# A product of 512 columns for the high and low parts of an activation, and side steps held in program order

## The chip, the cores and the metric

One core of a Trainium2 chip runs the whole program in one launch. The metric is the device time of an execution in microseconds (us). The kernel before takes 3224.32 us, the median of 3 runs (3224.06 to 3224.76). Engines are named as in the profile: PE is TensorE's products, PEld its loads of the stationary operand, DVE is VectorE, ACT is ScalarE, POOL is GpSimd and SP the engine that issues the loads.

## The reference

Two transformer blocks on 256 tokens of width 2048, all in float32. The first block is an SSD (Mamba-2) and an attention branch, then a product-key expert layer (`peer`): each token takes 8 heads x 16 of 16384 experts, found by a top-16 of the sums of two top-16 lists.

```python
def peer(h, wq, k1, k2, u, v):
    q = (t @ wq).reshape(T, PEER_HEADS, 2, PEER_KEY_DIM // 2)
    ...
    v1, i1 = lax.top_k(s1, PEER_TOPK)
    v2, i2 = lax.top_k(s2, PEER_TOPK)
    ...
    sc, pos = lax.top_k(cand, PEER_TOPK)
    g = jax.nn.softmax(sc, axis=-1)
    ...
        act = jax.nn.gelu(jnp.einsum('thkd,td->thk', u[ib], tb), approximate=False)
        return jnp.einsum('thk,thkd->td', gb * act, v[ib])
```

The second block is an attention with a relative bias from a table (`rel_bias`), a convolution branch, a cross attention on a memory of 256 rows (`mem`) and an MLP of 8192 hidden units, `square(relu(nm @ w1)) @ w2`.

## The kernel before

**Products.** A float32 product is made of three on rounded parts: each weight tile is split into a high part (`whi`, a cast by ACT, line 114) and a low part (`wlo`, the remainder, by DVE, line 115), the activation likewise (`hTh`, `hTl`), and high x high, high x low and low x high are summed in PSUM. One split covers 128 x 1024 weights; a raw tile of 1 MB is loaded by SP's queue into one of 3 buffers (`raw`) and gives two splits; `whi` and `wlo` have 3 buffers each.

**Two block forms.** `gemm_block` (line 147) holds 128 columns of the activation stationary and streams 512 weight columns. `gemm_cols` (lines 174 to 176) holds 128 weight columns stationary and streams the activation's 256 tokens: three products of 256 columns for each K tile and each 128 weight columns, in blocks of 512 weight columns, 192 products a block. It serves `up` of the expert layer (8 stages e of 4 blocks, all 16384 experts densely) and `w1` of the MLP (16 blocks). The token weights go in afterwards: `gate` multiplies the activations (written to DRAM as `act`, read back as `ag`) with a dense table of gate weights (`gd`, read in pieces of 64 bytes), and `down` is 8 stages of 4 `gemm_block`s.

**Order.** Blocks are written one after the other; work of other kinds is cut into steps (generators) and a rate says how many are put between the groups of a block (`step(rate)`): `routing` (top-16 steps, softmax, then the one-hot products of `all_gates`) beside `wq` and `up`, `gate(e+1)` beside `down(e)`, and `ahead` (squares of `mem`, the bias table) beside `down(2)`. `evac` moves a finished block out of PSUM. This written order is only the start: a scheduler orders each engine's instructions by its own estimate of when they can run, so a side step may land earlier than it is written.

**Names for the steps below.** `top16`, `route` (lines 788 to 838), `gate` (944 to 961), `fetch` (932, up to three pieces ahead), `ahead` (977 to 1000), the MLP's `f` (1359).

## Time and profile before

| | |
|---|---|
| median of 3 runs | 3224.32 us |
| the profiled execution | 3223.47 us, its span 3221.7 us |
| mean granted clock of TensorE | 0.997 |
| PE, PEld busy | 99%, 86% of the span |
| DVE, ACT busy | 62%, 47% |
| up and its gates | about 522 to 1283 us |
| down | about 1285 to 2020 us |
| MLP | about 2492 us to the end |

A busy PE is not a PE at its peak, since products overlap and their ends are modelled; the number of products that start in a stretch says more. The clock is given as a share of 2.4 GHz, with 1.2 GHz as its other level.

### The profile page before, as it was taken

To read this page: it belongs to the slowest core of one execution; us is meant where nothing else is said; L and a number is where in the kernel's file an instruction comes from. 1 tells how busy PE (TensorE), PEld (TensorE's weight loads), DVE (VectorE), ACT (ScalarE), POOL (GpSimd) and SP (SyncE) were. 2 spreads that over 40 slices of the span, in tenths; PEclk is the share of its full clock that TensorE was granted. 3 is DMA by queue.
4 is the path that set the end of the run, shared out by engine and by line. 5 is a ranking of instruction groups with operands and counts; after the bars stand their busy time and mean duration, and the time that the engine had idled before them with its cause. 6 is when DMAs were issued, how large, how long until landed. Compare 5 with 4: busy or idle time off the path is not lost.

```text
span 3221.7 us, 45786 instructions
## 1 busy us (share of the span) xinstructions
PE 3183.3 (99%) x18818; PEld 2766.7 (86%) x18818; DVE 2004.5 (62%) x2812; ACT 1529.6 (47%) x1967; POOL 92.2 (3%) x126
## 2 busy tenths in 40 slices
PE   8999999999999999999999999999999999999998
PEld 7877788999999999777787778888888989899897
DVE  6665679955666654555555555799666555555555
ACT  6456555544444444444443444545656434444344
POOL 0000000000000010000100000000000000000000
PEclk9999999999999999999999999999999999999999
DMA  6544454565667786667666765555554555555554
GB/s 234 183 144 171 144 180 157 200 209 203 229 240 248 242 289 214 233 235 239 231 223 228 240 215 183 196 183 177 176 170 170 185 189 189 183 186 189 187 183 157
DMA packets 101475, 647.31 MB, mean 201 GB/s; under 512 B 11269, under 2 KB 12421, under 8 KB 32400
## 3 DMA queue, kind: packets, MB, share of 16 engines
q1 hardware_dynamic: 82512, 575.63, 51.7%
q0 software_dynamic: 18752, 68.74, 6.4%
q8 instruction: 147, 2.41, 0.3%
q14 instruction: 64, 0.52, 0.0%
HBM read 607.11 MB, written 37.22 MB: 200 GB/s over the span
## 4 chain that ended last, share of the span: by engine, by line
PE 72%; issue 15%; DVE 6%; DMA 4%; POOL 1%; ACT 1%; SPq 0%; ACTq 0%; POOLq 0%; DVEq 0%
PE acc L147 52%; PE acc L176 5%; PE acc L174 5%; PE acc L175 5%; DMA ag<-gd 3%; DVE wlo L115 2%; PE tp L214 1%; DVE scr L793 0%; POOL gd L898 0%; DVE i L828 0%; PE mm L743 0%; DVE hTl L959 0%; DMA raw<-in_peer_v_dram 0%; DMA raw<-in_mem_dram 0%; POOL act L915 0%
## 5 line engine op out<-in xcount | busy, mean ns | idle before, releaser
L115 DVE TENSOR_TENSOR wlo<-raw,whi 128x1024 fp32r<-128x1024 f32 x1064 | 1300.1, 1223 | 1041.8 <-ACT whi L114 1038.1
L114 ACT CAST whi<-raw 128x1024 fp32r<-128x1024 f32 x1064 | 1114.6, 1049 | 1455.2 <-PE acc L147 853.0
L147 PE MATMUL acc<-whi,hTh 128*128 128x512 f32 x2650 | 1061.7, 401 | 10.5 <-ACT whi L114 10.5
L147 PE MATMUL acc<-wlo,hTh 128*128 128x512 f32 x2650 | 1051.5, 397 | 7.0 <-DVE wlo L115 6.8
L147 PE MATMUL acc<-whi,hTl 128*128 128x512 f32 x2650 | 1050.8, 397 | 0.0
L176 PE MATMUL acc<-hTh,wlo 128*128 128x256 f32 x3072 | 866.8, 282 | 10.1 <-DVE wlo L115 9.9
L174 PE MATMUL acc<-hTh,whi 128*128 128x256 f32 x3072 | 868.0, 283 | 0.0
L175 PE MATMUL acc<-hTl,whi 128*128 128x256 f32 x3072 | 863.6, 281 | 0.0
L147 PEld LDWEIGHTS acc<-whi,hTh 128*128 128x128 f32 x2650 | 498.7, 188 | 132.7 <-ACT whi L114 10.9
L147 PEld LDWEIGHTS acc<-wlo,hTh 128*128 128x128 f32 x2650 | 499.0, 188 | 129.0 <-DVE wlo L115 13.2
L147 PEld LDWEIGHTS acc<-whi,hTl 128*128 128x128 f32 x2650 | 498.4, 188 | 120.7 <-issue 0.3
L176 PEld LDWEIGHTS acc<-hTh,wlo 128*128 128x128 f32 x3072 | 579.4, 189 | 14.9 <-DVE wlo L115 14.4
L174 PEld LDWEIGHTS acc<-hTh,whi 128*128 128x128 f32 x3072 | 579.8, 189 | 0.2
L175 PEld LDWEIGHTS acc<-hTl,whi 128*128 128x128 f32 x3072 | 579.7, 189 | 0.2
L1087 DVE SCALAR_TENSOR_TENSOR cc<-hc,vec,cc 128x256 f32<-128x256 f32 x240 | 102.1, 478 | 0.5
L955 DVE TENSOR_TENSOR ag<-ag 128x1024 f32<-128x1024 f32 x32 | 39.2, 1225 | 61.5 <-DMA ag<-gd 61.2
L958 ACT CAST hTh<-ag 128x1024 fp32r<-128x1024 f32 x32 | 32.9, 1050 | 31.7 <-DVE ag L955 22.5
L675 DVE TENSOR_TENSOR x<-acc,x 128x512 f32<-128x512 f32 x72 | 46.4, 681 | 0.3 <-PE acc L147 0.2
L911 DVE TENSOR_TENSOR at<-acc,rtok 128x512 f32<-128x512 f32 x64 | 43.7, 690 | 0.5
L959 DVE TENSOR_TENSOR hTl<-ag,hTh 128x1024 fp32r<-128x1024 f32 x32 | 38.5, 1222 | 1.6 <-ACT hTh L958 0.8
L915 POOL DMA_DIRECT2D act<-at x32 | 17.4, 545 | 741.4 <-ACT at L913 741.1
L940 POOL DMA_DIRECT2D ag<-gd x32 | 37.4, 1170 | 6.3 <-DMA gd<-gs 5.1
(314 smaller groups left out, 1496.3 us busy)
## 6 DMA issues: line engine op xcount, KB each, us to landing
raw<-in_peer_u_dram SPq DMA_DIRECT2D x128, 1024.0 KB, 4.9
raw<-in_peer_v_dram SPq DMA_DIRECT2D x128, 1024.0 KB, 4.9
raw<-in_w_dram SPq DMA_DIRECT2D x128, 1024.0 KB, 4.9
raw<-in_w_in_dram SPq DMA_DIRECT2D x83, 1024.0 KB, 4.9
raw<-in_w_out_dram SPq DMA_DIRECT2D x32, 1024.0 KB, 4.9
raw<-in_wq_dram SPq DMA_DIRECT2D x16, 1024.0 KB, 4.9
act<-at POOLq DMA_DIRECT2D x32, 512.0 KB, 4.3
gd<-gs POOLq DMA_DIRECT2D x16, 1024.0 KB, 5.6
```

What stands on the lines that cost most here:

```text
L114: nc.scalar.copy(hi[:, :kt, :n], raw[:, k0 : k0 + kt, :n])
L115: nc.vector.tensor_sub(lo[:, :kt, :n], raw[:, k0 : k0 + kt, :n], hi[:, :kt, :n].bitcast(F32))
L147: mm(o, a, b, start=start, stop=stop)
L174: mm(o, hi[:, k, cs], xh[:, kk], start=kk == 0 and c % 2 == 0, stop=False)
L175: mm(o, hi[:, k, cs], xl[:, kk], start=False, stop=False)
L176: mm(o, lo[:, k, cs], xh[:, kk], start=False, stop=kk == 15 and c % 2 == 1)
L675: nc.vector.tensor_add(x[:, t, sl], acc[t], x[:, t, sl])
L911: nc.vector.tensor_mul(at[:, 2 * c : 2 * c + 2], acc[c], rt)
L940: nc.gpsimd.dma_start(g, gd[e, :, :, nb * 4 : nb * 4 + 4])
L955: nc.vector.tensor_mul(av, av, g.rearrange("p b c t -> p c b t"))
L959: nc.vector.tensor_sub(wl[:, cs], a, wh[:, cs].bitcast(F32))
L1087: nc.vector.scalar_tensor_tensor(o, hc[:, c, tap : tap + T], w[:, tap : tap + 1], o, OP.mult, OP.add)
```

## The change

The activation's high and low parts lie side by side (`hT`, [K tile, 2, 256]), so that one product of 512 columns under a stationary `whi` gives high x high in the left half of a PSUM bank and high x low in the right; `wlo` gives one product of 256 columns into the left half. A block now has 256 weight columns, and the weights of `peer_u` and `w1` are laid out for it on the host. `sums` adds the two halves at the block's end: ACT copies the right half out, DVE adds the left. Side steps are held in the order in which they are written (`pin`). The bias table is made by one product and spread over partitions by DMA, and two empty steps stand between mem's load and its squares.

```diff
+        pin = tc.keep_in_program_order
...
-        def gemm_cols(xh, xl, src, evac, rate=2):
+        def gemm_cols(x2, src, evac, rate=2):
...
-            for g in range(4):
+            for g in range(2):
                 raw = load_w(src(g))
                 for k0 in range(0, 4, 2):
-                    hi, lo = split_w(raw, k0)
-                    for k in range(2):
-                        kk = 4 * g + k0 + k
-                        for c in range(4):
+                    hi, lo = (
+                        a.rearrange("p a (k n) -> p (a k) n", n=T) for a in split_w(raw, k0)
+                    )
+                    for k in range(4):
+                        kk = 8 * g + 2 * k0 + k
+                        for c in range(2):
                             cs = slice(c * P, c * P + P)
-                            o = acc[c // 2][:, c % 2 * T : c % 2 * T + T]
-                            mm(o, hi[:, k, cs], xh[:, kk], start=kk == 0 and c % 2 == 0, stop=False)
-                            mm(o, hi[:, k, cs], xl[:, kk], start=False, stop=False)
-                            mm(o, lo[:, k, cs], xh[:, kk], start=False, stop=kk == 15 and c % 2 == 1)
+                            mm(
+                                acc[c], hi[:, k, cs], x2[:, kk].rearrange("p a t -> p (a t)"),
+                                start=kk == 0, stop=False,
+                            )
+                            mm(acc[c][:, :T], lo[:, k, cs], x2[:, kk, 0], start=False, stop=kk == 15)
...
+        def sums(o, acc):
+
+            for c in range(2):
+                nc.scalar.copy(o[:, c], acc[c][:, T:])
+                nc.vector.tensor_add(o[:, c], acc[c][:, :T], o[:, c])
...
         def new_hT():
-            h = main.tile([P, KD, T], F32R, name="hTh", tag="hTh", bufs=2)
-            l = main.tile([P, KD, T], F32R, name="hTl", tag="hTl", bufs=2)
-            return h, l
...
+            x2 = main.tile([P, KD, 2, T], F32R, name="hT", tag="hT", bufs=2)
+            return x2[:, :, 0], x2[:, :, 1], x2
...
-            nc.vector.max(vals[:, 0:8], src)
+            z.pin(nc.vector.max(vals[:, 0:8], src))
...
-            nc.vector.tensor_scalar_mul(mx, sc[:, 0:1], -1.0)
+            z.pin(nc.vector.tensor_scalar_mul(mx, sc[:, 0:1], -1.0))
...
-                    nc.vector.tensor_tensor(four(B2), io, row(i2T, t), OP.is_equal)
+                    z.pin(nc.vector.tensor_tensor(four(B2), io, row(i2T, t), OP.is_equal))
...
             for nb in range(4):
-                def f(acc, nb=nb):
-                    at = pp.tile([P, 4, T], F32, name="at", bufs=2)
-                    for c in range(2):
-                        nc.vector.tensor_mul(at[:, 2 * c : 2 * c + 2], acc[c], rt)
-                    yield
...
+                at = pp.tile([P, 4, T], F32, name="at", bufs=2)
+                for b in range(2):
+
+                    def f(acc, nb=nb, b=b, at=at):
+                        z.sums(at[:, 2 * b : 2 * b + 2], acc)
+                        yield
+                        nc.vector.tensor_mul(at[:, 2 * b : 2 * b + 2], at[:, 2 * b : 2 * b + 2], rt)
+                        if b:
+                            nc.scalar.activation(at, at, AF.Gelu)
...
-                nc.vector.tensor_mul(av, av, g.rearrange("p b c t -> p c b t"))
+                z.pin(nc.vector.tensor_mul(av, av, g.rearrange("p b c t -> p c b t")))
                 yield
                 cs = slice(nb * 4, nb * 4 + 4)
-                nc.scalar.copy(wh[:, cs], a)
+                z.pin(nc.scalar.copy(wh[:, cs], a))
...
                 mn = z.load_w(A["mem"][:, t].rearrange("p (a b) -> p a b", b=512))
+                yield
+                yield
                 for b in range(4):
-                    z.sq_sum(mn[:, b], ssm[:, t, b : b + 1])
+                    z.pin(z.sq_sum(mn[:, b], ssm[:, t, b : b + 1]))
                     yield
...
+            bv = pp.tile([8, 384], F32)
+            yield
+            pb = z.mm_tile()
+            z.pin(mm(pb[:8, :384], rb, bk, start=True, stop=True))
...
-            for h in range(8):
-                pb = z.mm_tile()
-                mm(pb[:, :384], rb[:, h : h + 1].to_broadcast([33, P]), bk, start=True, stop=True)
-                bv = pp.tile([P, 384], F32, name="bv", bufs=2)
-                nc.scalar.copy(bv, pb[:, :384])
-                nc.gpsimd.dma_start(env["bd"][h], bv)
+            for h in range(0, 8, 4):
+                br = pp.tile([P, 4, 384], F32, name="br", tag="at", bufs=2)
+                nc.gpsimd.dma_start(br, bd1[h : h + 4].partition_broadcast(P))
+                nc.gpsimd.dma_start(env["bd"][h : h + 4].rearrange("h p j -> p h j"), br)
                 yield
```

The MLP's `f` changes as `up`'s does (`sums`, then relu and scale, square, split), in halves.

What this makes of the engines' order, at the places that matter. PE in an up block before (`acc0`, `acc1` are PSUM banks, `hTh`, `hTl` the activation's parts):

```order
L174 MATMUL acc1_11578<-hTh_2976,whi_11701 128x256
L175 MATMUL acc1_11578<-hTl_2977,whi_11701 128x256
L176 MATMUL acc1_11578<-hTh_2976,wlo_11702 128x256
L174 MATMUL acc0_11577<-hTh_2976,whi_11729 128x256
L175 MATMUL acc0_11577<-hTl_2977,whi_11729 128x256
L176 MATMUL acc0_11577<-hTh_2976,wlo_11730 128x256
```

PE in an up block of the change:

```order
L182 MATMUL acc1_7772<-hT_2974,wlo_7776 128x256
L178 MATMUL acc0_7771<-hT_2974,whi_7796 128x512
L182 MATMUL acc0_7771<-hT_2974,wlo_7797 128x256
L178 MATMUL acc1_7772<-hT_2974,whi_7796 128x512
L182 MATMUL acc1_7772<-hT_2974,wlo_7797 128x256
```

Two products stand where three stood, of 512 and of 256 columns.

DVE beside the routing before (L791 to L795 and L835 to L837 are top-16 and softmax steps):

```order
L837 RECIPROCAL sm_p_4014<-sm_p_4014 128x1
L793 MATCH_REPLACE scr_3354<-v_p_4019,scr_3353 128x128
L824 TENSOR_TENSOR eq_p_3963<-abf_p_3961,iok_3351 128x512
L794 MAX v_p_4019<-scr_3354 128x8
L827 TENSOR_TENSOR eq_p_3963<-eq_p_3963,if_p_3897 128x512
L795 MAX_INDEX iu_p_4020<-v_p_4019,scr_3354 128x8
L828 TENSOR_REDUCE i12_3350<-eq_p_3963 128x2x16
L115 TENSOR_TENSOR wlo_3827<-raw_3824,whi_3826 128x1024
```

DVE beside the routing in the change (L804 to L808, L850 and L852 are those steps, L194 the adds of `sums`):

```order
L118 TENSOR_TENSOR wlo_4963<-raw_4960,whi_4962 128x1024
L852 RECIPROCAL sm_p_4942<-sm_p_4942 128x1
L804 MAX v_p_4947<-scr_3350 128x8
L805 MAX_INDEX iu_p_4948<-v_p_4947,scr_3350 128x8
L806 MATCH_REPLACE scr_3350<-v_p_4947,scr_3350 128x128
L807 MAX v_p_4947<-scr_3350 128x8
L118 TENSOR_TENSOR wlo_4984<-raw_4960,whi_4983 128x1024
L808 MAX_INDEX iu_p_4948<-v_p_4947,scr_3350 128x8
L194 TENSOR_TENSOR at_4836<-acc0_4837,at_4836 128x256
L194 TENSOR_TENSOR at_4836<-acc1_4838,at_4836 128x256
```

Two heads' steps are mixed before, and one head's follow one another now. Counted by `wlo`, the softmax steps (`mx_p`) stand from the 135th to the 183rd before and from the 140th to the 240th now; the number of table switches on ACT in this part goes from 8 to 22.

ACT at the end of an up block in the change (`L193` copies the right half of a bank, `L117` is the cast to `whi`):

```order
L117 CAST whi_7895<-raw_7893 128x1024
L911 COPY gs_7758<-mm_7816 128x128x4
L911 COPY gs_7758<-mm_7826 128x128x4
L117 CAST whi_7919<-raw_7893 128x1024
L193 COPY at_7646<-acc0_7771 128x256
L117 CAST whi_7961<-raw_7959 128x1024
L193 COPY at_7646<-acc1_7772 128x256
L117 CAST whi_7981<-raw_7959 128x1024
```

The block of `acc0_7771` ends with `whi_7858`; two casts of the next block stand ahead of the first copy, one between the copies. Before, ACT had none of these copies there.

DVE in the first down stage before (`ag` is multiplied with its gates on L955):

```order
L955 TENSOR_TENSOR ag_13440<-ag_13440 128x1024
L115 TENSOR_TENSOR wlo_13407<-raw_13404,whi_13406 128x1024
L959 TENSOR_TENSOR hTl_13368<-ag_13440,hTh_13367 128x1024
L115 TENSOR_TENSOR wlo_13423<-raw_13404,whi_13422 128x1024
L955 TENSOR_TENSOR ag_13552<-ag_13552 128x1024
L115 TENSOR_TENSOR wlo_13450<-raw_13447,whi_13449 128x1024
L115 TENSOR_TENSOR wlo_13466<-raw_13447,whi_13465 128x1024
L924 SCALAR_TENSOR_TENSOR x_1801<-acc0_13297,x_1801 128x512
L924 SCALAR_TENSOR_TENSOR x_1801<-acc1_13298,x_1801 128x512
L955 TENSOR_TENSOR ag_13698<-ag_13698 128x1024
```

DVE in the first down stage of the change (L973 is that multiplication, L977 the low part after it):

```order
L973 TENSOR_TENSOR ag_11706<-ag_11706 128x1024
L118 TENSOR_TENSOR wlo_12009<-raw_12006,whi_12008 128x1024
L118 TENSOR_TENSOR wlo_12025<-raw_12006,whi_12024 128x1024
L942 SCALAR_TENSOR_TENSOR x_1799<-acc0_11857,x_1799 128x512
L942 SCALAR_TENSOR_TENSOR x_1799<-acc1_11858,x_1799 128x512
L118 TENSOR_TENSOR wlo_12043<-raw_12040,whi_12042 128x1024
L118 TENSOR_TENSOR wlo_12059<-raw_12040,whi_12058 128x1024
L977 TENSOR_TENSOR hT_11634<-ag_11706,hT_11634 128x4x256
```

Counted by `wlo`, the four `ag` steps there (one of gate 1, three of gate 2) stand behind the 414th, 416th, 418th and 419th before; in the change those of gate 1 stand behind the 412th, 420th, 426th and 432nd. On ACT the squares of the first `mem` tile stand ahead of the casts of the raw tile loaded next; in the change they stand behind both of them.

## Rows read from the trace of the kernel before

**Rows 1.** The page, part 1: busy us and share of each engine.
```profile
PE 3183.3 (99%) x18818; PEld 2766.7 (86%) x18818; DVE 2004.5 (62%) x2812; ACT 1529.6 (47%) x1967; POOL 92.2 (3%) x126
```
**Rows 2.** The chain in order of time: start, length, what ("issue": no wait shown).
```profile
654.19 22.17 issue
676.91 22.18 issue
...
1563.09 1.48 PE mm L996 x4
...
2582.49 89.60 PE acc L147 x384
2762.97 89.60 PE acc L147 x384
```
**Rows 3.** Windows: each engine's busy us and instructions in a stretch, granted clock.
```profile
core 0: us, PE busy (x) PEld busy (x) DVE busy (x) ACT busy (x) POOL busy (x), PEclk, DMA share, GB/s
380.00:400.00 20.00, 20.00 (x94) 16.18 (x93) 12.84 (x16) 11.55 (x20) 0.00 (x0) 1.00 0.54 190
460.00:480.00 20.00, 20.00 (x96) 16.34 (x95) 20.00 (x72) 13.07 (x22) 0.00 (x0) 1.00 0.49 165
500.00:520.00 20.00, 18.17 (x87) 14.23 (x86) 19.90 (x71) 10.54 (x20) 0.00 (x0) 1.00 0.41 147
523.00:640.00 117.00, 109.96 (x890) 106.25 (x889) 111.52 (x338) 63.80 (x103) 2.19 (x4) 1.00 0.53 184
640.00:800.00 160.00, 160.00 (x1358) 159.95 (x1357) 84.47 (x84) 65.91 (x64) 3.72 (x7) 1.00 0.60 208
1160.00:1180.00 20.00, 17.14 (x132) 16.53 (x131) 13.38 (x13) 8.26 (x10) 5.38 (x7) 0.94 1.02 349
1330.00:1350.00 20.00, 16.33 (x64) 12.73 (x63) 8.30 (x7) 5.24 (x5) 0.00 (x0) 0.91 0.58 197
1510.00:1530.00 20.00, 16.80 (x60) 12.74 (x59) 9.58 (x9) 7.25 (x14) 0.00 (x0) 0.83 0.73 248
```
**Rows 4.** Waits of PE, 500 to 650 us: total us, times, longest.
```profile
PE acc L176 <- DVE wlo L115: 6.8, 12, 1.1
PE acc L147 <- DVE wlo L115: 1.8, 2, 1.6
```
**Rows 5.** Waits of PE, 1130 to 1900 us.
```profile
PE acc L147 <- DVE wlo L115: 5.0, 4, 3.7
PE acc L176 <- DVE wlo L115: 3.1, 4, 2.2
PE acc L147 <- ACT whi L114: 2.7, 1, 2.7
```
**Rows 6.** Groups by line and shape: busy us, mean ns, idle before and releaser.
```profile
L174 PE MATMUL acc<-hTh,whi 128*128 128x256 f32 x3072 | 868.0, 283 | 0.0
L911 DVE TENSOR_TENSOR at<-acc,rtok 128x512 f32<-128x512 f32 x64 | 43.7, 690 | 0.5
L996 PE MATMUL mm<-bk,rb 33*128 33x384 f32 x16 | 6.5, 515 | 0.0
L836 ACT ACT_TABLE_LOAD x4 | 5.1, 1283 | 0.1
L1328 DVE TENSOR_TENSOR x<-x,gf 128x512 f32<-128x512 f32 x6 | 3.9, 683 | 0.0
L1130 ACT ACTIVATE uv<-acc,rstd 128x256 f32<-128x256 f32 x8 | 3.8, 474 | 3.8 <-PE acc L147 3.8
L1185 DVE TENSOR_TENSOR hTl<-mm,hTh 128x256 fp32r<-128x256 f32 x8 | 3.3, 419 | 0.5 <-ACT hTh L1184 0.5
```
**Rows 7.** Timeline of DVE, 1285 to 1345 us: start, length, [idle before <- releaser].
```profile
1316.78 1.23 DVE L955 TENSOR_TENSOR ag<-ag 128x1024 f32<-128x1024 f32 x1 [3.13 <-DMA ag<-gd]
...
1335.19 1.22 DVE L955 TENSOR_TENSOR ag<-ag 128x1024 f32<-128x1024 f32 x1 [6.34 <-DMA ag<-gd]
1336.33 3.49 DVE L115 TENSOR_TENSOR wlo<-raw,whi 128x1024 fp32r<-128x1024 f32 x3
```
**Rows 8.** Timeline of ACT, 1495 to 1545 us.
```profile
1516.70 0.63 ACT L251 ACTIVATE junk<-raw 128x512 f16<-128x512 f32 x1 [7.58 <-DMA raw<-in_mem_dram]
```
**Rows 9.** The page, part 6: DMA issues, KB each, median us to landing.
```profile
raw<-in_peer_v_dram SPq DMA_DIRECT2D x128, 1024.0 KB, 4.9
```
**Rows 10.** Timeline of SP's queue, 1505 to 1517 us.
```profile
1505.62 0.33 SPq L108 DMA_DIRECT2D raw<-in_mem_dram  x1
```

More of the change, by code (lines that the diff above doesn't have):

```diff
@@ L195, in new_hT, with scratch @@
         def new_hT():
-            h = main.tile([P, KD, T], F32R, name="hTh", tag="hTh", bufs=2)
-            l = main.tile([P, KD, T], F32R, name="hTl", tag="hTl", bufs=2)
-            return h, l
-        def scratch(shape, tag):
-            return main.tile(shape, F32, name="scr", tag=tag, bufs=2)
+            x2 = main.tile([P, KD, 2, T], F32R, name="hT", tag="hT", bufs=2)
+            return x2[:, :, 0], x2[:, :, 1], x2
+        def scratch():
+            return main.tile([P, 2, KD * T], F32, name="scr", tag="hT", bufs=2)
         def tp_tile():
@@ L284, in front @@
     with phase_pool(tc, "ssd", True) as sp:
-        xh, xl = z.new_hT()
-        xT = z.scratch([P, KD, T], "hTh")
+        xh, xl, _ = z.new_hT()
+        xT = z.scratch()[:, 0].rearrange("p (k t) -> p k t", t=T)
         def load_x(k0, n):
@@ L760, in peer @@
         nc.vector.tensor_copy(iok, C["iota"][:, :16].unsqueeze(2).to_broadcast([P, 16, 16]))
-        sall = z.scratch([P, 2, 16, P], "hTh")
-        scr = z.scratch([P, 4, 4 * T], "hTl")
+        both = z.scratch()
+        sall = both[:, 0].rearrange("p (t h k) -> p t h k", t=2, h=16)
+        scr = both[:, 1].rearrange("p (a b) -> p a b", a=4)
         k12s = scr[:, 2].rearrange("p (a b c) -> p a b c", a=2, b=4)
@@ L806, in route @@
             cd = scr[:, 3, T : 2 * T].rearrange("p (a b) -> p a b", b=16)
-            nc.vector.tensor_add(
-                cd,
-                v[:, 0].unsqueeze(2).to_broadcast([P, 16, 16]),
-                v[:, 1].unsqueeze(1).to_broadcast([P, 16, 16]),
+            z.pin(
+                nc.vector.tensor_add(
+                    cd,
+                    v[:, 0].unsqueeze(2).to_broadcast([P, 16, 16]),
+                    v[:, 1].unsqueeze(1).to_broadcast([P, 16, 16]),
+                )
             )
@@ L907, in up @@
             for nb in range(4):
-                def f(acc, nb=nb):
-                    at = pp.tile([P, 4, T], F32, name="at", bufs=2)
-                    for c in range(2):
-                        nc.vector.tensor_mul(at[:, 2 * c : 2 * c + 2], acc[c], rt)
-                    yield
-                    nc.scalar.activation(at, at, AF.Gelu)
-                    acts[e, nb] = z.dram.tile([P, 4, T], F32, name="act%d_%d" % (e, nb))
-                    nc.gpsimd.dma_start(acts[e, nb], at)
-                    yield
-                z.gemm_cols(th, tl, lambda g: A["peer_u"][e * 4 + nb, g], f, rate)
+                at = pp.tile([P, 4, T], F32, name="at", bufs=2)
[6 more added lines that the diff above has]
+                            nc.scalar.activation(at, at, AF.Gelu)
+                            acts[e, nb] = z.dram.tile([P, 4, T], F32, name="act%d_%d" % (e, nb))
+                            nc.gpsimd.dma_start(acts[e, nb], at)
+                        yield
+                    z.gemm_cols(z.th2, lambda g: A["peer_u"][e * 8 + nb * 2 + b, g], f, rate)
         def add(nb):
@@ L1023, in peer @@
         sb = main.tile([P, 2, 4], F32, name="ssb", bufs=1)
-        nh, nl = z.new_hT()
+        nh, nl, _ = z.new_hT()
         def fin(nb):
@@ L1065, in second @@
     with phase_pool(tc, "mix2") as fp:
-        mh, ml = z.new_hT()
+        mh, ml, _ = z.new_hT()
         def src(nb):
@@ L1354, in second, with f @@
         for q in range(4):
-            hh, hl = z.new_hT()
+            hh, hl, _ = z.new_hT()
             for nb in range(4):
-                def f(acc, nb=nb, hh=hh, hl=hl):
-                    sb = fp.tile([P, 4, T], F32, name="hid", bufs=2)
-                    for c in range(2):
-                        nc.vector.scalar_tensor_tensor(sb[:, 2 * c : 2 * c + 2], acc[c], 0.0, rt6[0], OP.max, OP.mult)
-                    yield
-                    nc.scalar.activation(sb, sb, AF.Square)
-                    yield
-                    cs = slice(nb * 4, nb * 4 + 4)
-                    nc.scalar.copy(hh[:, cs], sb)
-                    nc.vector.tensor_sub(hl[:, cs], sb, hh[:, cs].bitcast(F32))
-                    yield
-                z.gemm_cols(fh, fl, lambda g: A["w1"][q * 4 + nb, g], f)
+                sb = fp.tile([P, 4, T], F32, name="hid", bufs=2)
+                for b in range(2):
+                    def f(acc, nb=nb, b=b, sb=sb, hh=hh, hl=hl):
+                        o = sb[:, 2 * b : 2 * b + 2]
+                        z.sums(o, acc)
+                        yield
+                        nc.vector.scalar_tensor_tensor(o, o, 0.0, rt6[0], OP.max, OP.mult)
+                        nc.scalar.activation(o, o, AF.Square)
+                        yield
+                        cs = slice(nb * 4 + 2 * b, nb * 4 + 2 * b + 2)
+                        nc.scalar.copy(hh[:, cs], o)
+                        nc.vector.tensor_sub(hl[:, cs], o, hh[:, cs].bitcast(F32))
+                        yield
+                    z.gemm_cols(fh2, lambda g: A["w1"][q * 8 + nb * 2 + b, g], f)
             for nb in range(4):
@@ L1455, in layout @@
     A["wo_c"] = tiles(I["wo_c_2"][0])
-    A["w1"] = tiles(I["w1_2"][0])
+    w = I["w1_2"][0].reshape(2, 8, P, 32, 256).transpose(3, 0, 2, 1, 4)
+    A["w1"] = np.ascontiguousarray(w).reshape(32, 2, P, 4, 512)
     A["w2"] = tiles(I["w2_2"][0])
```

27 lines of the change are left out of this document (15 added, 12 removed).

## Prediction

> **What bounds the kernel now.** I read the page's engine totals first: TensorE is busy 99% of the span, VectorE 62%, ScalarE 47% [rows 1]. A busy TensorE need not issue at its best rate, so next I read the chain of waits in order of time, where long pieces without a break give that rate. Four blocks of `gemm_block` are one piece of 384 products of 512 columns in 89.60 us [rows 2], 233.3 ns each. Between the end of one such piece (2582.49 + 89.60 = 2672.09) and the next (2762.97) lie 90.88 us, and in them four blocks of `gemm_cols`: 4 x 192 = 768 products of 256 columns, 118.33 ns each. One up block starts 22.72 us after the other (654.19, 676.91), 192 products, 118.33 ns again. There TensorE runs without a gap; ScalarE's and VectorE's splitting of the weights lies wholly beside it.
>
> Third, windows: how many products start in a stretch, against that rate. 640 to 800 holds 1358, and 160 / 0.11833 is 1352: full. 523 to 640 holds 890 where 989 would fit, so 99 x 0.11833 = 11.7 us are lost; 500 to 520 holds 87 where the full 380 to 400 holds 94, 1.6 us [rows 3]. The list of waits names the cause: TensorE waits for VectorE's `wlo` 14 times, 8.6 us [rows 4], while VectorE is busy 111.5 of 117 us [rows 3] with the routing's top-16 steps between the splits. The same count gives 4.4 us lost in 1160 to 1180 (132 of 169), 5.1 in 1330 to 1350 (64 of 85.7 at 512 columns) and 6.0 in 1510 to 1530 (60 of 85.7): 15.5 us, with a mean granted clock of 0.94, 0.91 and 0.83, so part of each ran at the lower level, 1.2 GHz, right after a stop of TensorE [rows 3, 5]. Two causes: VectorE stands 3.13 and 6.34 us for the transfer `ag<-gd` with the next `wlo` behind it [rows 7], and ScalarE stands 7.58 us for the `mem` tile with the next `whi` behind it [rows 8].
>
> **The change part by part.**
>
> *One product of 512 columns for two of 256.* Per 128 weight columns and K tile, 3 x 118.33 = 355.0 ns become 233.3 + 118.33 = 351.7 ns: 3.33 ns less, since the columns stay 768 and only one product's own fixed part goes. The row of the lines counts 3072 such triples [rows 6]: 3072 x 3.33 = **10.2 us** saved. No row shows the two widths alternating. Bounds: 0 if an alternating pair costs what its columns cost; 15 if the stationary load that goes too was holding something (I add half the gain again). I take 10.2, as both rates were measured back to back on full stretches. The Trainium skill, "TensorE: Matmul & The Clock Gate", section "Back-to-back issue gap", gives a gap of N/2.4 + 2.5 ns; by it the saving is 3072 x 2.5 = 7.7 us. The trace's 118.33 and 233.3 are both longer than that rule's 109.2 and 215.8, so the measured pair goes into my sum.
>
> *New work at each block's end.* A pair of half blocks now has 4 ScalarE copies out of PSUM (474 ns, the nearest row, `uv<-acc` 128x256) and 4 VectorE adds (419 ns, `hTl<-mm` 128x256); the two multiplications by `rtok` stay, now SBUF to SBUF (683 against 690) [rows 6]. That is 1.9 us of ScalarE and 1.7 of VectorE per 22.5 us of products. In quiet up stretches VectorE is busy 84 of 160 and ScalarE 66 [rows 3], so these hide. In order: ScalarE's second copy stands between two `whi`, VectorE's add behind it, then the multiplication, then the next `wlo`. From the block's end that chain is at worst 1.05 (`whi`) + 0.47 + 0.42 + 0.68 + 1.22 = 3.85 us, and TensorE holds two finished splits of 8 x 0.3517 = 2.81 us, 5.6 us. Nobody waits; I cost it at 0, with 1.75 us of slack. Bounds: 0 to the slow rival below. The 96 boundaries themselves cost TensorE nothing before: the full stretches above contain them.
>
> *Bias table.* 16 products of 33x384 (two passes for each of 8 heads) [rows 6] become 2. Four take 1.48 us on the chain [rows 2], 0.37 each: 14 x 0.37 = **5.2 us** saved. Added: two reads of 786 KB beside the same amount written, all on POOL's queue, where the next gate fetches stand behind them; three pieces are fetched ahead, so those wait for nothing. Bounds 0 (if that stretch turns out to wait for transfers) to 5.2.
>
> *Routing pinned.* Its VectorE work stays about the same, but the order spreads it from the 140th `wlo` to the 240th, where it was packed between the 135th and the 183rd. I estimate the routing at 94 us: in 523 to 640, 111.5 busy less 37 splits x 1.22 and some 7 us of `at` leaves 59; 500 to 520 holds 19.9 less 7 x 1.22, 11 in 20 us, and at that density the 63 us from 460, where VectorE becomes full, to 523 add 35 [rows 3]. Over 100 splits x 2.81 = 281 us VectorE then has 122 (splits) + 94 + 33 (22 half blocks with adds and multiplications) = 249, 89% where it was 95%. Not idle, but behind TensorE's pace no more. Bounds: 13.3 us recovered (all of it) to 0, or a loss if VectorE's handshakes with ScalarE now hold up `wlo` over the longer stretch; I take **10.3**. ScalarE switches tables 22 times in place of 8 (from the order) at 1.28 us [rows 6], 18 us over 281; it is about half busy and stays ahead.
>
> *Gating pinned.* VectorE's `ag` steps stand 4 to 8 `wlo` apart instead of four within six, so a fetch has some 17 us to land and VectorE meets landed data; the four fetches of one down stage no longer fall together. The losses at 1160 and 1330 (9.5 us) should go but for about 1. Bounds 0 to 9.5.
>
> *Mem tile.* The first square now stands behind one more raw tile's two splits, whose transfer was issued later than mem's, so ScalarE meets a landed tile. What is late next: mem holds one of three raw buffers longer, and the stream runs on two. A raw load lands in 4.9 us at the median [rows 9], but this mem load took 11.1 (1505.62 to 1516.70) [rows 8, 10]; two buffers bear about 8. So of the 6.0 us I leave 3. Bounds 0 to 6. Gate and mem together: 15.5 - 4 = **11.5 us**.
>
> *The shared tag* of high and low part and the moved scratch change when slots come free, but the order outside the peer and MLP parts is nearly the same as before; I cost it at 0.
>
> Sum: 10.2 + 5.2 + 10.3 + 11.5 = 37.2. The profiled execution took 3223.47 us (span 3221.7), 0.85 below the median of the three runs: 3223.47 - 37.2 + 0.85 = **3187 us**.
>
> **Rivals.**
> 1. *VectorE stays short.* The pins only stretch the shortage: the adds and the longer routing keep VectorE in step with nothing to spare, and half of the fetch stalls move. For it: 89% by my own count, and in-order waits on ScalarE inside each routing step. Against: TensorE needs a `wlo` only every 2.81 us and holds two. Then only 10.2 + 5.2 + 5.7 come off: 3203 us.
> 2. *Products cost their columns alone.* 768 before, 768 now. The first term is 0: 3197 us. Against: the same columns took 90.88 us in 768 products and 89.60 us in 384 [rows 2]. The same page of the Trainium skill, section "Step-by-step: what each phase is for", says throughput is "purely `N cycles`"; by it this rival is the case, and the trace does not agree, by 3.33 ns a product.
> 3. *Slower: ScalarE's queue stops at each block's end.* A copy waits there for the block's last product, and every later `whi` stands behind it. If the splits done ahead do not cover the chain, TensorE stops at each of the 96 half-block ends. It decides against the change from 37/96 = 0.39 us a stop on. With one finished split ahead instead of two the stop is 3.85 - 2.81 = 1.0 us, 96 us in all: 3283 us. For it: in the routing stretch other steps lie between. Against: the order puts two splits ahead of every first copy, and blocks of `wq` end with ScalarE copies of 0.68 us out of PSUM too (380 to 400 full at 94 products). The skill's same page, section "Architectural detail: the array is 16× 32×32, not 1× 128×128", calls ScalarE and VectorE strict first-in first-out; the trace's `wlo` behind a waiting `ag` [rows 7] agrees.
>
> **How the numbers follow.** Forecast 0.66, rival 1 0.17, rival 2 0.08, rival 3 0.05, no visible effect from several small offsets 0.04. A measurement of this kernel tells about 0.2% (6.4 us) from no change. Faster: 0.66 + 0.17 + 0.08 = 0.91; slower 0.05; same 0.04. Low end: all bounds, 15 + 5.2 + 13.3 + 15.5 = 49, 3175, and 2 us for stalls too small to be listed: 3173. High end: rival 1 with its gate share gone, 3209, less 1: 3208.
>
> **What would show it.** Right: four w1 blocks' worth of products in about 90.0 us for 90.88; no wait of TensorE over 1 us in 523 to 640, and VectorE busy shares of some 85 to 90% until about 780; no drop of the granted clock near 1330; two products of 33x384 for 16. Wrong: 512 and 256 alternating at 355 ns a pair; TensorE waiting for `whi` behind a copy `at<-acc`, every 11.3 us; VectorE at 95% and more over all of 460 to 780; a stop of over 3 us around the mem tiles.

## The result, and the profile after

The changed kernel takes 3175.08 us (median of 4 runs, 3172.84 to 3175.69), the kernel before beside it 3224.19 us: a ratio of 0.9847, interval 0.983 to 0.9864. That is 49.1 us less, where 37.2 were forecast; the time lies at the low end of the range. The profiled execution took 3172.84 us, 50.6 under the one before.

The page of the changed kernel, part 1 (busy us, share, instructions) and the first line of part 4 (share of the chain that ended last, by engine):

```profile
PE 3152.0 (99%) x15732; PEld 2606.3 (82%) x15732; DVE 2084.6 (66%) x3020; ACT 1605.7 (51%) x2198; POOL 91.1 (3%) x123
...
PE 99%; ACT 1%; DMA 0%; DVE 0%; issue 0%; ACTq 0%; SPq 0%
```

TensorE has 3086 products fewer than in [rows 1], 3072 from the merged product and 14 from the bias table. VectorE does 80 us more and ScalarE 76, the sums at the blocks' ends above all, and neither is on the chain. Windows of the changed kernel, the stretches of [rows 3] (busy us and instructions by engine, then the granted clock):

```profile
core 0: us, PE busy (x) PEld busy (x) DVE busy (x) ACT busy (x) POOL busy (x), PEclk, DMA share, GB/s
460.00:480.00 20.00, 20.00 (x96) 16.34 (x95) 15.16 (x37) 12.79 (x18) 0.00 (x0) 1.00 0.46 162
500.00:520.00 20.00, 20.00 (x98) 16.57 (x97) 13.93 (x36) 10.10 (x17) 0.00 (x0) 1.00 0.47 164
523.00:640.00 117.00, 117.00 (x672) 101.93 (x671) 103.92 (x263) 72.29 (x109) 2.19 (x4) 1.00 0.57 198
640.00:800.00 160.00, 160.00 (x921) 138.96 (x920) 144.21 (x335) 98.97 (x141) 3.83 (x8) 1.00 0.59 207
1160.00:1180.00 20.00, 20.00 (x115) 17.40 (x114) 11.69 (x14) 9.39 (x12) 0.56 (x1) 1.00 0.66 227
1330.00:1350.00 20.00, 20.00 (x87) 16.09 (x86) 12.50 (x12) 9.25 (x9) 1.70 (x2) 1.00 0.68 237
1510.00:1530.00 20.00, 20.00 (x87) 15.51 (x85) 10.10 (x11) 11.12 (x16) 0.00 (x0) 1.00 0.70 258
```

Every window in which TensorE was short before is full now, at a clock of 1.00, and VectorE is no longer at its limit: 20.00 of 20 us became 15.16, and from 523 to 800 us it works 89 to 90% of the time. The waits of TensorE from 1130 to 1900 us (total us, times, longest), three rows and 10.8 us in [rows 5], are one row:

```profile
PE acc L150 <- DVE wlo L118: 0.2, 1, 0.2
```

The waits of VectorE in that stretch, first the kernel before, then the changed one; the prediction does not use these rows:

```profile
DVE wlo L115 <- ACT whi L114: 273.5, 184, 3.3
DVE ag L955 <- DMA ag<-gd: 61.2, 29, 6.3
```

```profile
DVE wlo L118 <- ACT whi L117: 302.2, 249, 4.2
DVE at L194 <- ACT at L193: 6.6, 10, 0.7
```

VectorE stood 61.2 us for gate pieces, in 29 stops; it now stands for none. (Its long wait for `whi` is the pace of the stream: ScalarE's `whi` waits for TensorE to leave its buffer, 70.3 us from 1440 to 1600 us alone.)

Starts of products in the two traces give TensorE's whole loss. An interval's kind is the line of its product and of the next one; what an interval has above the median of its kind, where that is 50 ns or more, is called a stop here. The stops add up to 64.2 us before and 30.4 after. So 33.8 us of stops went. From 500 to 640 us it is 14.8 (15.6 to 0.8), from 1140 to 1900 us 20.5 (21.0 to 0.5, of which 6.4 to 0.4 at the mem tile, 1480 to 1530 us); around 2200 to 2300 us 2.5 came new (2.6 to 5.1).

The chain in order of time (start, length, what), the changed kernel's w2 blocks:

```profile
2537.89 89.59 PE acc L150 x384
2716.23 89.60 PE acc L150 x384
2894.59 89.60 PE acc L150 x384
```

Between two of them lie the four w1 blocks: 2716.23 - 2627.48 = 88.75 us, where before there were 90.88 and 90.03 were forecast. That is 346.7 ns a pair of products, 8.3 under the old triple in place of 3.3, which would make 25.6 us over 3072 triples. It does not: the other stretches run slower, as the experiments show.

### The profile page after: what moved, and what is told of

Its sections match the earlier page's. It is cut to its first block, busy times and chain, and to the rows that moved or that the text cites. A ratio compares the mean times of both kernels' runs of the same rounds, so it can differ in the third digit from the quotient of the medians.

```text
span 3171.1 us, 39979 instructions
## 1 busy us (share of the span) xinstructions
PE 3152.0 (99%) x15732; PEld 2606.3 (82%) x15732; DVE 2084.6 (66%) x3020; ACT 1605.7 (51%) x2198; POOL 91.1 (3%) x123
## 4 chain that ended last, share of the span: by engine, by line
PE 99%; ACT 1%; DMA 0%; DVE 0%; issue 0%; ACTq 0%; SPq 0%
PE acc L150 60%; PE acc L178 23%; PE acc L182 11%; PE tp L226 1%; PE mm L909 1%; PE mm L755 0%; PE mm L647 0%; PE tp L746 0%; PE mm L794 0%; PE mm L569 0%; ACT junk L263 0%; PE mm L644 0%; PE mm L756 0%; PE mm L1200 0%; ACT whi L117 0%; DMA raw<-in_peer_v_dram 0%
## 5 line engine op out<-in xcount | busy, mean ns | idle before, releaser
L117 ACT CAST whi<-raw 128x1024 fp32r<-128x1024 f32 x1064 | 1115.0, 1048 | 1288.6 <-PE acc L150 890.8
L150 PE MATMUL acc<-whi,hT 128*128 128x512 f32 x5300 | 1701.0, 398 | 7.6 <-ACT whi L117 7.6
L150 PEld LDWEIGHTS acc<-whi,hT 128*128 128x128 f32 x5300 | 993.9, 188 | 248.3 <-ACT whi L117 7.6
L178 PE MATMUL acc<-hT,whi 128*128 128x512 f32 x3072 | 1086.2, 397 | 0.0
L150 PE MATMUL acc<-wlo,hT 128*128 128x512 f32 x2650 | 1049.1, 396 | 1.2 <-DVE wlo L118 1.2
L182 PE MATMUL acc<-hT,wlo 128*128 128x256 f32 x3072 | 863.4, 281 | 0.0
L178 PEld LDWEIGHTS acc<-hT,whi 128*128 128x128 f32 x3072 | 576.6, 188 | 136.3
L150 PEld LDWEIGHTS acc<-wlo,hT 128*128 128x128 f32 x2650 | 497.9, 188 | 119.4 <-DVE wlo L118 3.1
L182 PEld LDWEIGHTS acc<-hT,wlo 128*128 128x128 f32 x3072 | 578.9, 188 | 0.4 <-DVE wlo L118 0.2
L193 ACT COPY at<-acc 128x256 f32<-128x256 f32 x128 | 48.0, 375 | 82.3 <-PE acc L182 82.3
L194 DVE TENSOR_TENSOR at<-acc,at 128x256 f32<-128x256 f32 x128 | 53.6, 419 | 20.0 <-ACT at L193 19.5
L193 ACT COPY hid<-acc 128x256 f32<-128x256 f32 x64 | 23.9, 373 | 48.3 <-PE acc L182 48.3
L194 DVE TENSOR_TENSOR hid<-acc,hid 128x256 f32<-128x256 f32 x64 | 26.9, 421 | 21.0 <-ACT hid L193 21.0
L977 DVE TENSOR_TENSOR hT<-ag,hT 128x1024 fp32r<-128x1024 f32 x32 | 38.9, 1216 | 0.0
L973 DVE TENSOR_TENSOR ag<-ag 128x1024 f32<-128x1024 f32 x32 | 38.9, 1216 | 0.0
```

Of the source, the lines that this page charges most:

```text
L117: nc.scalar.copy(hi[:, :kt, :n], raw[:, k0 : k0 + kt, :n])
L150: mm(o, a, b, start=start, stop=stop)
L178: mm(acc[c], hi[:, k, cs], x2[:, kk].rearrange("p a t -> p (a t)"), start=kk == 0, stop=False,)
L182: mm(acc[c][:, :T], lo[:, k, cs], x2[:, kk, 0], start=False, stop=kk == 15)
L193: nc.scalar.copy(o[:, c], acc[c][:, T:])
L194: nc.vector.tensor_add(o[:, c], acc[c][:, :T], o[:, c])
```

## Experiments

e4 ran once; the others have an interval. Differences are of medians to 3175.08 us. A ratio's interval is some 0.0015 either way, 5 us, so single differences under 10 us are rough. The kernel before took 3223.55 us beside e1 to e4, 3224.86 beside e5 to e8 and 3225.48 beside e9 to e12, where it took 3224.19 beside the changed kernel: up to 1.3 us of a difference can come from that.

**e1, the merged product undone.**

```diff
-    mm(acc[c], hi[:, k, cs], x2[:, kk].rearrange("p a t -> p (a t)"), start=kk == 0, stop=False)
+    mm(acc[c][:, :T], hi[:, k, cs], x2[:, kk, 0], start=kk == 0, stop=False)
+    mm(acc[c][:, T:], hi[:, k, cs], x2[:, kk, 1], start=False, stop=False)
```

> The changed kernel with the 512-column product under whi taken apart into two of 256 under the same stationary columns (three of 256 per 128 weight columns and K tile, as before); blocks of 256, sums at the block's end, order and bias table stay. Theory A (the whole gain of 8.33 ns a triple seen in the w1 stretch, 88.75 us against 90.88 for 256 triples, comes from the wide product): products of 256 start 118.33 ns apart again, four w1 blocks take 90.9 us, and the time rises by 3072 x 8.33 = 25.6 us to 3200.7 us. Theory B (the wide product saves only its own fixed part, 3.33 ns a triple, and the rest came with the half blocks or with the operand's new layout): four w1 blocks take 89.6 us, and the time rises by 10.2 us to 3185.3 us.

3183.25 us (3182.79 to 3185.17), ratio 0.9876 (0.9861 to 0.9892): 8.2 us more. The chain of e1, from the end of one w2 piece to the next: 2723.09 - 2632.21 = 90.88 us, 355.0 ns a triple again, as theory A has it. But the total rises by 8.2, near theory B's 10.2. Both had a part: w1's gain is all the merged product's, and it is not the gain elsewhere.

```profile
2542.61 89.60 PE acc L150 x384
2723.09 89.60 PE acc L150 x384
```

**e3, e4: eight and eight; the wide product alone.** e3 issues the eight wide products of a split and then its eight narrow ones; e4 leaves the narrow one out.

```diff
 e3
-    for k in range(4):
-        for c in range(2):
+    for part in range(2):
+        for k in range(4):
+            for c in range(2):
...
 e4
-    mm(acc[c][:, :T], lo[:, k, cs], x2[:, kk, 0], start=False, stop=kk == 15)
```

> The changed kernel with the products of a split in another order: first its eight of 512 columns under whi, then its eight of 256 under wlo, in place of one of each in turn. Columns, stationary loads and products are the same in number. Theory A (it is the turn of a long and a short product that makes the pair cheaper than the two apart): 512 after 512 costs 233.3 ns and 256 after 256 118.3, 351.7 a pair save at one border in eight: four w1 blocks take 89.9 us and the time rises by some 13 us to 3188 us. Theory B (the pair is cheaper because a triple has two stationary loads in place of three, or because of the layout of the moving operand): four blocks stay at 88.75 us, the time within 2 us of 3175.

> The changed kernel with the 256-column product under wlo left out of the blocks of weight columns (the low part of the weights doesn't enter those results). It shows what the product of 512 columns costs when only its own kind stands beside it. Theory A (the turn of long and short makes it cheaper): 233.3 ns from start to start within a split, as in the blocks of w2. Theory B (with activations as the moving operand the product of 512 columns is shorter by itself): 229.2 ns, as in the changed kernel. The time itself falls by up to 3072 x 117.4 ns = 361 us, less where transfers or the splitting of weights then set the pace.

e3: 3173.59 us (3172.38 to 3176.18), the same as the changed kernel. But its w1 takes 2715.00 - 2624.98 = 90.02 us in the chain, 351.6 ns a pair: theory A on the w1 stretch, where the last three quarters lose 1.3 us each, and theory B on the total. So the changed kernel must be losing elsewhere what w1 gains.

```profile
2535.38 89.60 PE acc L150 x384
...
2715.00 89.60 PE acc L150 x384
```

The chain of e4 shows one quarter of w1 with 256 wide products in 59.73 us, 233.3 ns each, the rate of the blocks of w2 (theory A). Activations as the moving operand do not make the wide product shorter. (2893.57 us in all.)

```profile
2346.00 89.60 PE acc L150 x384
2435.61 59.73 PE acc L178 x256
```

The starts in the changed kernel's trace give the answer. Strict turns, a wide product and a narrow one one after the other, have two steady rhythms. In w1's last three quarters a pair takes 229 + 117.7 = 346.7 ns; in nearly all of the up stages, and in the first quarter of w1, two pairs take 229 + 117 + 240 + 121 ns, 353.4 a pair. A rhythm lasts until a short stop of TensorE, or the entry into a quarter of w1, sets it anew; the slow one held for up to 670 pairs in a row. Of 2959 pairs seen whole, 2079 are in the slow rhythm, 831 in the fast one and 49 in neither: 351.5 ns for the first two together, 3.5 under 355.0, and 3072 x 3.5 = 10.8 us. That agrees with e1 and with the forecast's 10.2. The stops' 33.8 us, these 10.8 and 14 products of the bias table at 0.37 us, 5.2, make 49.8 of the 50.6 us between the two profiled executions.

**e5, e6, e12, e7: other orders.** e5: two wide ones, then two narrow. e6: the second bank's pair turned round. e12: one pair in eight turned round. e7: in the blocks of 512 columns each part for both banks in turn.

```diff
 e5
+    for part in range(2):
         for c in range(2):
...
 e6
+    if c and kk:
+        two.reverse()
...
 e12
+    if c and k == 3:
+        two.reverse()
...
 e7
+    for three in zip(*now):
         for o, a, b, start, stop in three:
```

> The changed kernel with the products of one K tile in another order: the two of 512 columns (one into each PSUM bank), then the two of 256, in place of long and short for the first bank, then for the second. In the trace of the changed kernel the pair of long and short keeps one of two rhythms, 346.7 ns (the last three quarters of w1) or 353.4 ns (nearly all of the up stages, the first quarter of w1), until a short stop changes it; 2079 of 2959 pairs seen keep the slow one. Theory A (strict turns of long and short have two stable rhythms, any order with neighbours alike has one, as eight and eight had with 351.6 ns): 351 to 352 ns a pair everywhere, four w1 blocks 90.0 us, time 3172 to 3175 us. Theory B (the extra time comes from two products in a row into one bank): with the banks in turn the slow rhythm goes, 346.7 ns or less everywhere, four w1 blocks 88.75 us, time 2079 x 6.7 ns = 14 us under 3175, 3161 us.

> The changed kernel with the second bank's pair turned round: 512, 256 for the first bank, then 256, 512 for the second (but for the first K tile of a block), so that products of one width stand two by two, each two of 256 in different banks. Theory A (strict turns alone have two rhythms): one rhythm of 351 to 352 ns a pair in up and w1 alike, time 3172 to 3175 us. Theory B (which rhythm holds is settled by the entry, whatever the order): w1's last three quarters keep 346.7 and the up stages 353.4, time within 2 us of 3175. Theory C (two products in a row into one bank cost more): as A or worse, since here too each bank gets its two in a row.

> The changed kernel with one pair in eight turned round: the last of each split has its 256-column product first, so that at each split's border two of 512 stand side by side. Strict turns kept whichever rhythm a stretch began in (346.7 or 353.4 ns a pair); at w1 the three quarters that began in the slow one came 233 ns after the last product before, the ones in the fast one 227 or 232. Theory A (the turned pair throws the dice again at every split, and the fast rhythm is met more often than now, where 28 in 100 pairs have it): 349 to 350 ns a pair, 3167 to 3171 us. Theory B (every order but strict turns comes out at the same mean, as the three orders before did with 351.1 to 351.9): 351 to 352 ns, 3173 to 3176 us. Theory C (the turn leads into the slow rhythm each time): 353 ns, 3180 us.

> The changed kernel with the blocks of products of 512 columns (w2, peer_v, w_in and the others) in another order: the three products of a K tile no longer three in a row into one bank, but each part for both banks in turn, xh whi, xh whi, xh wlo, xh wlo, xl whi, xl whi. Theory A (the bank of the neighbour doesn't matter to a product of 512 columns): 233.3 ns from start to start as before, 384 products in 89.60 us, time within 2 us of 3175. Theory B (three products in a row into one bank hold each other up): they fall to the 229.2 ns that the long product shows in the pair's faster rhythm, 384 in 88.0 us, and the time falls by 7978 x 4.1 ns = 33 us to 3142 us.

e5 took 3173.58 us (3173.2 to 3175.14), e6 3174.58 (3172.69 to 3175.72), e12 3177.57 (3177.0 to 3177.91), e7 3174.48 (3173.62 to 3175.36). None differs from the changed kernel by 0.2%. The chains of e6 and of e12 have w1 as a piece of 512 products between pieces of w2:

```profile
2537.22 89.58 PE acc L150 x384
2626.80 89.94 PE acc L185 x512
2716.75 89.58 PE acc L150 x384
2806.33 89.94 PE acc L185 x512
```

```profile
2537.45 89.60 PE acc L150 x384
2627.05 90.29 PE acc L185 x512
2717.34 89.60 PE acc L150 x384
```

e6 has one rhythm, 89.94 / 256 = 351.3 ns a pair; e5 has about 351.3 by its starts, in up and w1 alike. For both, theory A holds. e12 has 352.7, between theories B and C: w1's fast rhythm went, and the up stages gained nothing for it.

e7's 384 products keep 89.60 us, so the bank of the neighbour does not matter to them (theory A). Its chain shows both rhythms in one place of one program, with w1 code that did not change:

```profile
2537.49 89.60 PE acc L153 x384
2717.53 89.59 PE acc L153 x384
2895.87 89.60 PE acc L153 x384
```

The first gap is 2717.53 - 2627.09 = 90.44 us, 353.3 ns a pair, the second 2895.87 - 2807.12 = 88.75, 346.7. Windows of e7 inside the two quarters count 455 products in 80 us, then 463:

```profile
2630.00:2710.00 80.00, 80.00 (x455) 69.49 (x454) 48.42 (x55) 40.92 (x56) 0.00 (x0) 1.00 0.53 188
2810.00:2890.00 80.00, 80.00 (x463) 70.34 (x462) 49.86 (x57) 42.13 (x57) 0.00 (x0) 1.00 0.54 188
```

VectorE, ScalarE and the transfers are alike in both and the clock is 1.00. Nor does the place in the program settle it: e8 runs up from 634 to 781 us, 421 pairs, in the fast rhythm, where the changed kernel runs the slow one from 533 to 771 us. By the starts, the slow quarters of e7, e8 and e9 began 233 ns after the last product before, the fast ones of the kernels with strict turns 226 to 232. The Trainium skill, "TensorE: Matmul & The Clock Gate", section "Back-to-back issue gap", says that the spacing of products is set by the loads of the stationary operand as well as by the products. The rows give a load 188 ns (below); but in the kernel before, products of 256 columns with a load each started 118.33 ns apart, so loads overlap. No run here parts loads and products, and what sets the rhythm stays open. A load's row, the changed kernel:

```profile
L182 PEld LDWEIGHTS acc<-hT,wlo 128*128 128x128 f32 x3072 | 578.9, 188 | 0.4 <-DVE wlo L118 0.2
```

**e2, e8, e9, e10: the pins taken out**, all of them (e2), the routing's (e8), the gate pieces' (e9), and those of mem with its two empty steps (e10).

```diff
 e2
-    pin = tc.keep_in_program_order
+    pin = lambda i: i
 e8
-    z.pin(nc.vector.max(vals[:, 0:8], src))
+    nc.vector.max(vals[:, 0:8], src)
...
 e9
-    z.pin(nc.vector.tensor_mul(av, av, g.rearrange("p b c t -> p c b t")))
+    nc.vector.tensor_mul(av, av, g.rearrange("p b c t -> p c b t"))
...
 e10 (and e2)
-    yield
-    yield
     for b in range(4):
 e10
-        z.pin(z.sq_sum(mn[:, b], ssm[:, t, b : b + 1]))
+        z.sq_sum(mn[:, b], ssm[:, t, b : b + 1])
```

> The changed kernel without any of the pins of side steps and without the two empty steps ahead of the squares of mem, so that the scheduler packs the routing again (its VectorE work lies between the 92nd and the 147th group of rows of wlo where the pins spread it to the 186th). Theory A (the three stalls of before are worth what they took there, 13.3 for the routing, 9.5 for the gate pieces, 5.5 for mem, and they come back whole): time rises by about 28 us to 3203 us, with TensorE waiting for wlo between 460 and 640. Theory B (the new sums at the block's end are more work for a VectorE that is short again, so the packed routing stalls longer than before): over 3210 us. Theory C (the half blocks spread the steps by themselves, so that the pins are worth little): below 3187 us.

> The changed kernel with the five pins of the routing alone taken out (those of its top-16 steps, candidate sums, index shifts, softmax and one-hot steps); the gate pieces, the squares of mem and the bias table stay pinned. Theory A (each stall stands for itself): the stalls of TensorE between 500 and 640 us come back, 13.3 to 14.8 us, and nothing else: 3189 us. Theory B (the routing's place in the order decides where the gate pieces and mem fall, so that most of the 32 us that all pins together are worth hangs on it): over 3195 us, with waits for wlo after 1130 us as well. Theory C (with the gate steps pinned the packed routing costs less than it did before): under 3183 us.

> The changed kernel with the two pins of the gate pieces alone taken out (the multiplication on VectorE, the high part's copy on ScalarE); routing, mem and bias table stay pinned. Theory A (the stalls that the trace of before shows near 1160 and 1330 are all that these pins remove): 9.5 us come back, 3184.6 us. Theory B (unpinned gate steps stall in more places than the two that I listed: with all pins out TensorE stood some 11 us between 1140 and 1420 and 6 between 1600 and 1900): 15 to 18 us, over 3189 us. Theory C (with the routing spread and half blocks, gate pieces meet landed data anyway): under 3179 us.

> The changed kernel without the two empty steps and the pins at the squares of mem; all else stays. Theory A (the whole stop of before comes back, 6.0 us near 1510): 3181 us, with ScalarE standing some 7 us at the mem tile. Theory B (as in my forecast the later squares keep a raw buffer and cost half of what they save): 3178 us. Theory C (what stalls there hangs on the gate steps around it, not on the squares): within 2 us of 3175.

e2: 3207.22 us (3204.96 to 3210.18), ratio 0.9949 (0.9936 to 0.9963), 32.1 more; between theories A and B, 4 over A. e8: 3184.74 us (3183.79 to 3189.28), 9.7 more: between A's 3189 and C's 3183, and B is out. e9: 3195.95 us (3194.46 to 3197.14), ratio 0.9909 (0.9894 to 0.9924), 20.9 more: theory B, and over its 15 to 18, twice A's 9.5. e10: 3175.55 us (3172.93 to 3176.7), 0.5 more: theory C. The three parts make 31.1 of the 32.1. By starts, as in the section on the result, e8 has 12.8 us of stops from 500 to 640 us where the changed kernel has 0.8; from 1140 to 1900 us e9 has 22.2 and e10 1.9, where the changed kernel has 0.5.

Waits of TensorE, 450 to 1900 us, in e8, then 1130 to 1900 us in e9:

```profile
PE acc L182 <- DVE wlo L118: 5.8, 10, 1.3
PE acc L150 <- DVE wlo L118: 2.1, 3, 1.6
```

```profile
PE acc L150 <- DVE wlo L118: 11.7, 8, 2.1
PE acc L182 <- DVE wlo L118: 2.9, 3, 2.1
```

Windows of e8, the routing's stretch, and of e9, the stretch near mem:

```profile
523.00:640.00 117.00, 111.06 (x623) 94.18 (x622) 116.25 (x357) 71.93 (x123) 2.19 (x4) 1.00 0.55 186
```

```profile
1500.00:1600.00 100.00, 97.72 (x410) 77.09 (x409) 56.48 (x53) 46.42 (x58) 9.95 (x13) 0.98 0.78 282
```

Each cause is back by itself. In e8 VectorE is full again, 116.25 of 117 us, with waits like those of [rows 4]; only 0.3 us of them comes after 1130 us. In e9 the routing stretch stays full and VectorE stands for gate pieces once more:

```profile
DVE ag L973 <- DMA ag<-gd: 61.6, 28, 4.3
```

That is as much as the 61.2 us of the kernel before. These waits reach TensorE in eleven of its own, of up to 2.1 us, spread over 1130 to 1900 us, with a granted clock of 0.98 in the window above. But they are not the stops of the kernel before over again: outside the mem tile that one had 14.6 us of stops from 1140 to 1900 us, and it was full from 1600 to 1700 us, where e9 is not (the kernel before, then e9):

```profile
1600.00:1700.00 100.00, 100.00 (x430) 80.23 (x429) 59.87 (x54) 42.15 (x41) 8.52 (x10) 1.00 0.72 246
1600.00:1700.00 100.00, 98.00 (x414) 78.36 (x413) 55.74 (x51) 39.88 (x39) 6.84 (x8) 0.98 0.65 222
```

So e9's 20.9 us is what the pins are worth in the finished kernel, more than what they took out of the kernel before. With all pins out ScalarE stands at the mem tile as in [rows 8]; with mem alone unpinned it stands 3.6 us in place of 9.2. The waits of ScalarE, 1440 to 1600 us in e2 and 1440 to 1560 us in e10:

```profile
ACT junk L263 <- DMA raw<-in_mem_dram: 9.2, 2, 7.1
```

```profile
ACT junk L263 <- DMA raw<-in_mem_dram: 3.6, 2, 2.2
```

TensorE still stops once in e10 behind the second mem tile's squares, at 1499 us; its wait for `wlo` there, from 1130 to 1900 us the only row:

```profile
PE acc L150 <- DVE wlo L118: 0.8, 1, 0.8
```

By starts that stop is 1.7 us, against 0.4 us near there in the changed kernel. So with the gate steps pinned the mem edit is worth some 1.3 us of stops, too little for the medians to tell, and not the 6.0 of before. Whether it would be worth the 6 us without the gate pins was not tried alone: from 1480 to 1530 us, e9, in which it stands, has 1.8 us of stops, and e2, in which the routing's pins are out too, 3.6.

**e11, the bias table of before** (products for eight heads, not pinned).

```diff
-    z.pin(mm(pb[:8, :384], rb, bk, start=True, stop=True))
+    for h in range(8):
+        mm(pb[:, :384], rb[:, h : h + 1].to_broadcast([33, P]), bk, start=True, stop=True)
...
```

> The changed kernel with the bias table as before: a product of 33x384 for each of eight heads (16 passes in place of 2), eight copies out of PSUM, no round trip of the 8 rows, and not pinned. Theory A (products at the rate of the chain): 14 x 0.37 = 5.2 us more, 3180.3 us. Theory B (the copies on ScalarE and their place in its queue cost more than the products): over 3183 us. Theory C (that stretch waits for something else anyway): within 2 us of 3175.

3181.49 us (3179.43 to 3181.97), 6.4 more: nearest to theory A. The rows of the lines, e11 and then the changed kernel:

```profile
L1016 PE MATMUL mm<-bk,rb 33*128 33x384 f32 x16 | 6.5, 515 | 0.0
```

```profile
L1015 PE MATMUL mm<-bk,rb 33*8 33x384 f32 x2 | 0.8, 484 | 0.0
```

No version beat the changed kernel by more than the measurement tells.

## Why the prediction was right, and where its sizes were off

The direction and the likeliest case held, and the range, at its low end. The terms, in us; the second column is read from the traces of the two kernels (stops and pairs by starts, the bias table at 0.37 us a product), the third from the runs that undo one edit in the changed kernel:

```
term             forecast   gone in the trace   undone on its own
merged product     10.2          10.8                8.2   (e1)
bias table          5.2           5.2                6.4   (e11)
routing pinned     10.3          14.8                9.7   (e8)
gate pieces         8.5          14.5               20.9   (e9)
mem tile            3.0           6.0                0.5   (e10)
other stops         0            -1.5
sum                37.2     49.8 of 50.6       45.7 of 49.1
```

That the range held has luck in it. Its low end, 3173 us, put every term at its own bound, and two terms went past theirs: the routing 14.8 for at most 13.3, gate pieces and mem 20.5 for at most 15.5. The merged product stayed 4 us under its 15, and new stops elsewhere took 1.5 back.

- *Merged product*: the size held, and one sign named for it did not: w1 at about 90.0 us. The forecast took a fixed part of each width, 233.3 and 118.33, as if it did not depend on the neighbour. Orders with like neighbours give just that sum, 351.7 (351.3 to 351.7 in e3, e5, e6); strict turns give 346.7 or 353.4, and their mean here is 351.5. The term was right for a reason that is only half of the story.
- *Block ends at no cost*: held. In the waits of TensorE over the whole changed kernel the blocks have one row for `whi`, a single wait in the first 60 us, so none behind a copy:

```profile
PE acc L150 <- ACT whi L117: 7.6, 1, 7.6
```

  The kernel before had 48 such boundaries (32 blocks of up, 16 of w1), not the 96 that the prediction says cost nothing before; 96 is the new kernel's number. The copies were cheaper than assumed, the adds as assumed (rows of the lines of the changed kernel):

```profile
L193 ACT COPY at<-acc 128x256 f32<-128x256 f32 x128 | 48.0, 375 | 82.3 <-PE acc L182 82.3
L194 DVE TENSOR_TENSOR at<-acc,at 128x256 f32<-128x256 f32 x128 | 53.6, 419 | 20.0 <-ACT at L193 19.5
```

- *Routing*: held, with VectorE at 89 to 90% where 89 was worked out. In the trace the whole stop went, 14.8 us, 1.5 over the bound of 13.3; e8 brings 12.0 of it back by starts, and its time 9.7. Part of the difference is that e8 met the fast rhythm more often, 1041 pairs against 831, 210 x 6.7 ns = 1.4 us.
- *Gate pieces*: the step that failed in size. "The losses at 1160 and 1330 (9.5 us) should go but for about 1" counted only the two stops that showed as long waits. Outside mem the kernel before lost 14.6 us from 1140 to 1900 us: 11.5 at those two places, where the windows had counted 9.5, and 3.1 in small stops. The row that lists the places is VectorE's own, 61.2 us in 29 stops, each a possible stop of TensorE wherever the finished splits do not last. It does not give the size: much the same row (61.6 us) stands beside 22.2 us of TensorE's stops in e9.
- *Mem tile*: the mechanism was right for ScalarE and most of the credit was not the edit's. ScalarE meets a landed mem tile, as forecast: the changed kernel has no wait for it from 1440 to 1600 us. But with the gate steps pinned, all but some 1.3 us of the stop stays away without the mem edit too (e10), so most of the 6.0 us is not its doing. With all pins out (e2) 3.6 us of stops stand there, so the other pins have a part; how, no run shows. Two raw buffers, for which 3 us were left, cost TensorE nearly nothing: ScalarE stood for raw tiles in the changed kernel, and its window 1500 to 1600 us has TensorE busy 99.84 of 100 us.

```profile
1486.66 2.00 ACT L117 CAST whi<-raw 128x1024 fp32r<-128x1024 f32 x2 [3.97 <-DMA raw<-in_peer_v_dram]
...
1505.05 2.00 ACT L117 CAST whi<-raw 128x1024 fp32r<-128x1024 f32 x2 [4.94 <-DMA raw<-in_peer_v_dram]
```

```profile
1500.00:1600.00 100.00, 99.84 (x427) 79.18 (x426) 56.40 (x54) 43.88 (x51) 7.84 (x11) 1.00 0.72 258
```

By stops alone: the forecast listed 28.8 us in three causes and held back 7 of them in case. The trace lost 33.8. So 7 us of caution and 5 of stops that the windows did not count (1.5 beside the routing, 5.0 later, less 1.5 that came new elsewhere) make the 12 between forecast and time. Rival 2 (columns alone) is out by e1's w1 stretch, 90.88 us for the same columns in 768 products against 88.75 to 90.44 in 512. Rivals 1 and 3 are out by the waits, of which only 0.2 us are left from 1130 to 1900 us and none from 450 to 650.

## What to carry to other kernels

Where one engine feeds the bound one, read every wait of the feeder for its transfers, not only the waits that show on the bound engine: they name the places that can stop it. Their sum is not the loss: some 61 us of VectorE's waits cost TensorE 14.6 us in one order and about 22 in another. Undo each edit alone in the finished kernel; two edits that cure one stop (here mem's) can't be told apart by where the stop was. And what an edit undone gives back need not be what it took out. A rate measured with like neighbours is the rate of that order only, so price a new mixture with bounds on both sides.

## What the runs showed of the hardware

- Products of 512 and 256 columns in strict turns run in one of two steady rhythms, 346.7 or 353.4 ns a pair, in the same code, and stay in it for whole quarters of w1 (256 pairs) and longer. What sets it is open. If every slow pair of the changed kernel ran in the fast rhythm, 2079 x 6.7 ns = 14 us more would go, an estimate from its trace. None of the orders tried forces it: two and two, mirrored, eight and eight, one turned in eight give 351.3 to 352.7.
- The order of PSUM banks among products of 512 columns is worth nothing: 233.3 ns each in e7 as before, three in a row into one bank or in turn.
- Copies of 128x256 out of PSUM on ScalarE took 375 ns as plain copies, where the scaled ones of [rows 6] took 474.
